# Seven products in place of eight for two blocks of each channel mixer in a four-layer decoder trunk

## The chip, the cores and the metric

The kernel runs on one core of one Trainium2 chip. The metric is device time in microseconds (us) of one launch. Five engines work from queues of their own: TensorE (PE in the profile; its weight loads are PEld), VectorE (DVE), ScalarE (ACT), GpSimd (POOL, unused here) and SyncE (SP), which issues the transfers. Each takes its instructions in the order in which the kernel recorded them.

## The reference

Four layers over 256 tokens of width 1024. Each has a mixer (retention, dilated attention, gated MLP, retention again), the channel mixer that the change touches, and a gated embedding:

```
FFN_HIDDEN = -(-(8 * D_MODEL) // (3 * 256)) * 256        # 2816
def _swiglu(h, w_in, w_out):
    gate, up = jnp.split(h @ w_in, 2, axis=-1)
    return (jax.nn.silu(gate) * up) @ w_out
...
    f = _swiglu(_rmsnorm(h, norm_g[i, 2]), ffn_w_in[i], ffn_w_out[i])
    h = h + _rmsnorm(f.astype(h.dtype), norm_g[i, 3])
```

All inputs are fp32.

## The kernel before

Every weight is streamed once, in "chunks" of at most 128x1024 fp32; a transfer brings two chunks (1 MB) into one of four raw buffers (`RAWS`). `split_one` splits a chunk into a high part `wh` (ScalarE copies it to fp32r, L172) and a low part `wl` (VectorE subtracts, L173). Eight split chunks can live at once (`SLOTS`). Each product is then three matmuls, `mm3` (L202 to L204): high by high, and the two crossed terms, the part not streamed being the activation's own split pair (`a_hi`, `a_lo`).

What order the work has is written by hand in the program (a manual schedule). When `Chunk` hands chunk c to TensorE's code, `tick` records the split of chunk c+6 (`LEAD`) at that place in ScalarE's and VectorE's queues.

In the channel mixer, `ffn`, the first 512 columns of gate and of up are computed token by feature, then turned by transposes (`turn`). The other 2304 columns of each go in nine "pairs" i = 2 to 10 of 256 columns: two gate chunks and two up chunks of 24 matmuls each, which stream the 256 tokens past weight blocks (`feature_major`), then `hidden` (silu(gate)*up and its split: L927, L928, L930, L933, L934), then two chunks of the output weight, `rows` of pair i-2, with 12 matmuls of 512 columns each into the accumulators `acc`.

Of the kernel before, what the change touches and what calls it, by code (L numbers as in the profile page):

```python
# [9 lines left out]
F32 = mybir.dt.float32  # L10
# [14 lines left out]
RAWS = 4  # L25
# [24 lines left out]
def _size(d):  # L50
    return d[3] * sum(n for _, n in d[4])


def _plan(l):
    kind, j = l % 3, l // 3
    emb = _rows("ple_w_proj", l, 0, 2)
    mix = []
    if kind == 0:
        for h in range(4):
            mix += _cols("ret_w_in", j, 2048 + 512 * h, 512, 2)  # L60
            mix += _blocks("ret_w_in", j, 256 * h, 2) + _blocks("ret_w_in", j, 1024 + 256 * h, 2)
# [20 lines left out]
    for i in range(2, NPAIR):  # L82
        mix += _blocks("ffn_w_in", l, 256 * i, 2) + _blocks("ffn_w_in", l, HID + 256 * i, 2)
        mix += _rows("ffn_w_out", l, 2 * i - 4, 2)
    mix += _rows("ffn_w_out", l, 2 * NPAIR - 4, 4)
    for q in range(2):
        mix += _cols("ple_w_gate", l, 512 * q, 512, 2)
    return mix


PLANS = [_plan(l) for l in range(DEPTH)]


def _pack(l, w):
# [12 lines left out]
def trunk(ctx: ExitStack, tc: tile.TileContext, x, p_t, norm_g, gcols, wts, rel_bias, gm_ln, gm_ws, gm_bs,  # L107
# [14 lines left out]
        return (psum if tag == "ps" else accp).tile([128, 512], F32, tag=tag, name=tag)  # L122


    chunks, groups = [], []
    for l in range(DEPTH):
        off = 0
        for d in PLANS[l]:
            n = _size(d)
            if len(chunks) % 2 == 0:  # L130
                groups.append((2 * n, wts[l][off:off + 256 * n].rearrange("(p n) -> p n", p=128)))
            assert 2 * n == groups[-1][0]
            chunks.append((d, n))
            off += 128 * n
    raws, slots, released = {}, {}, set()
    st = {"load": 0, "split": 0, "take": 0, "rate": 2}

    def load_to(i):
        while st["load"] <= min(i, len(groups) - 1):
# [4 lines left out]
            for cs in (slice(0, n // 2), slice(n // 2, n)) if g == 1 else (slice(0, n),) if g else ():  # L144
                dma.dma_start(out=t[:, cs], in_=src[:, cs])
            st["load"] += 1

# [16 lines left out]
    def split_one():  # L164
        c = st["split"]
        assert can_split()
        load_to(c // 2 + RAWS - 1)
        n = chunks[c][1]
        raw = raws[c // 2][:, c % 2 * n:(c % 2 + 1) * n]
# [15 lines left out]
    class Chunk:  # L185
        def __init__(self, name):
            c = st["take"]
            d, n = chunks[c]
# [9 lines left out]
            released.add(self.c)  # L198


    def mm3(ps, lh, ll, rh, rl, start, stop):
        pe.matmul(ps, lhsT=lh, rhs=rh, start=start, stop=False)  # L202
        pe.matmul(ps, lhsT=lh, rhs=rl, start=False, stop=False)  # L203
        pe.matmul(ps, lhsT=ll, rhs=rh, start=False, stop=stop)  # L204


    ident = const.tile([128, 128], F32, name="ident")
# [233 lines left out]
    def retention(l, r, between, env):  # L441
# [14 lines left out]
        for hd in range(4):  # L456
# [47 lines left out]
            def scores():  # L504
# [388 lines left out]
        return late, acc  # L893

    def rel_vectors(rp):
        rel = rp.tile([32, 48], F32, name="rel")
        hot = rp.tile([32, 3, 384], F32, name="hot")
        band = rp.tile([16, 3, 384], F32, name="band")
        sb = rp.tile([16, 3, 384], F32, name="relv")
        rh, rl = (rp.tile([32, 48], F32R, name=t) for t in ("relh", "rell"))  # L900
        dma.dma_start(out=rel, in_=rel_bias)
        dma.dma_start(out=hot, in_=c_onehot)
        dma.dma_start(out=band, in_=c_mask)

        def compute():
            hr = rp.tile([32, 3, 384], F32R, name="hotr")
            act.activation(out=hr, in_=hot, func=AF.Copy)
            act.activation(out=rh, in_=rel, func=AF.Copy)
            dve.tensor_tensor(out=rl, in0=rel, in1=rh.bitcast(F32), op=ALU.subtract)
            for g in range(3):  # L910
                ps = ps_tile()
                for i, part in enumerate((rh, rl)):
                    pe.matmul(ps[0:16, 0:384], lhsT=part[:, cut(g, 16)], rhs=hr[:, g, :], start=i == 0, stop=i == 1)
                dve.tensor_tensor(out=sb[:, g, :], in0=ps[0:16, 0:384], in1=band[:, g, :], op=ALU.add)  # L914
            dma.dma_start(out=vec.rearrange("g h u -> h g u"), in_=sb)

        return compute


    def ffn(l, r, between, env):  # L920
# [30 lines left out]
            return ps  # L951

        def first(tt, gp, up):
            s = fp.tile([128, 512], F32, tag="s0", name="s0")
# [7 lines left out]
        u1 = second_half(wu)  # L962
        first(1, g1, u1)
        st["rate"] = P["rate"]
        h0 = [fp.tile([128, 4, 256], F32R, tag=f"h0{i}", name="h0") for i in range(2)]
        acc = None
        for i in range(2, NPAIR):
            gp = feature_major(name)
            if i == 2:
                spread(r)  # L970
                for tt in range(2):
                    turn(hid0[tt], h0[0], h0[1], 0, tt)
                hids[0], hids[1] = (h0, 0), (h0, 2)
                gain = load_gain(l, 3)
                if l == 0:
                    rel_part = rel_vectors(fp)
            if i == 5 and l == 0:
                rel_part()
            up = feature_major(name)
            hidden(i, gp, up)  # L980
            if acc is None:
                acc = new_acc()
            late = []
            z, k0 = hids[i - 2]
            for k in range(2):
                c = Chunk(wout)
                if i < NPAIR - 1:
                    row(c, z, k0 + k, acc, i == 2 and k == 0, False)
                    c.release()
                else:  # L990
                    row(c, z, k0 + k, acc, False, False, (0,))
                    late.append((c, z, k0 + k))
        for i in range(NPAIR - 2, NPAIR):
            z, k0 = hids[i]
            for k in range(2):
                c = Chunk(wout)
                row(c, z, k0 + k, acc, False, i == NPAIR - 1 and k == 1, (0,))
                late.append((c, z, k0 + k))
        return close_branch(late, acc, gain, r, l, 4)

    def embed_gate(l, r, between):
# [59 lines left out]
    with tc.manual_schedule():  # L1061
        dma.dma_start(out=ident, in_=c_ident)
        for tt in range(2):
            dma.dma_start(out=h[:, tt, cut(0)], in_=x[tok(tt), cut(0)])
            if tt == 0:
                dma.dma_start(out=gc, in_=gcols)
        load_to(0)
# [5 lines left out]
        load_to(RAWS - 1)  # L1073
        dve.memset(ones, 1.0)
        dve.memset(eps, EPS)
        act.preload_act_table(AF.Sqrt)
# [102 lines left out]
```

## Time and profile before

| | |
|---|---|
| time, median of 3 runs | 1721.83 us (1721.56 to 1721.88) |
| the profiled execution | 1721.27 us, its span 1719.5 us |
| TensorE busy | 1708.8 us, 99% of the span |
| VectorE busy | 1138.7 us, 66% |
| ScalarE busy | 980.9 us, 57% |
| mean granted TensorE clock | 0.999 |

The span runs from the first to the last instruction; 1.8 us of the profiled execution lie outside it. Busy shares are averages over the whole program.

### The profile page before, as it was taken

How to read it: one execution, taken by the hardware profiler on the slowest of the kernel's cores; microseconds unless marked ns; L12 is line 12 of the kernel's file. 1: busy time of each engine (PE TensorE's matmuls, PEld its weight loads, DVE VectorE, ACT ScalarE, POOL GpSimd, SP SyncE). 2: the span in 40 equal slices, each digit the busy share in tenths (PEclk: the TensorE clock that was granted, in tenths of full speed). 3: DMA queues.
4: the chain of work that ended last, by engine and by line, in shares of the span. 5: the costliest groups of instructions: out<-in, count | busy, mean ns of one | idle time of the engine just before them, and what ended most of it. 6: DMA issues, size and time to landing. Idle time of an engine off the chain costs nothing.

```text
span 1719.5 us, 26156 instructions
## 1 busy us (share of the span) xinstructions
PE 1708.8 (99%) x10667; PEld 1543.6 (90%) x10667; DVE 1138.7 (66%) x1663; ACT 980.9 (57%) x1506; POOL 0.2 (0%) x4
## 2 busy tenths in 40 slices
PE   9999999999999999999999999999999999999999
PEld 7888899998999999799998888899988888889997
DVE  7666665557888888765557676755567665675556
ACT  6545764447777777754447644644457555764435
POOL 0000000000000000000000000000000000000000
PEclk9999999999999999999999999999999999999999
DMA  8544465553656556455554754565544544555550
GB/s 291 221 170 173 172 225 179 184 191 131 208 160 183 165 168 180 147 204 181 196 172 147 277 194 149 191 213 187 181 168 166 198 173 172 189 208 200 178 194 25
DMA packets 53593, 314.22 MB, mean 183 GB/s; under 512 B 5633, under 2 KB 13617, under 8 KB 19169
## 3 DMA queue, kind: packets, MB, share of 16 engines
q1 hardware_dynamic: 53472, 312.56, 53.0%
q8 instruction: 83, 1.36, 0.3%
q14 instruction: 38, 0.30, 0.1%
HBM read 311.41 MB, written 1.12 MB: 182 GB/s over the span
## 4 chain that ended last, share of the span: by engine, by line
PE 93%; DVE 3%; ACT 2%; issue 1%; DMA 0%; SPq 0%; ACTq 0%; DVEq 0%
PE ps L204 20%; PE ps L202 20%; PE ps L203 20%; PE acc L202 7%; PE acc L204 7%; PE acc L203 7%; PE ps L326 2%; DVE wl L173 2%; PE ps L322 2%; PE ps L323 2%; PE acc L260 1%; PE ps L251 1%; PE acc L635 1%; ACT wh L172 1%; PE acc L597 0%
## 5 line engine op out<-in xcount | busy, mean ns | idle before, releaser
L173 DVE TENSOR_TENSOR wl<-raw,wh 128x1024 fp32r<-128x1024 f32 (+1 forms) x567 | 660.9, 1205 | 197.9 <-ACT wh L172 197.1
L172 ACT ACTIVATE wh<-raw 128x1024 fp32r<-128x1024 f32 (+1 forms) x567 | 564.3, 1040 | 176.0 <-PE ps L203 106.8
L202 PE MATMUL ps<-a_hi,wh 128*128 128x256 f32 x1792 | 509.5, 284 | 0.0
L204 PE MATMUL ps<-a_hi,wl 128*128 128x256 f32 x1792 | 507.0, 283 | 0.0
L203 PE MATMUL ps<-a_lo,wh 128*128 128x256 f32 x1792 | 507.0, 283 | 0.0
L202 PEld LDWEIGHTS ps<-a_hi,wh 128*128 128x128 f32 x1792 | 343.6, 192 | 1.9 <-DVE relv L914 0.4
L203 PEld LDWEIGHTS ps<-a_lo,wh 128*128 128x128 f32 x1792 | 343.7, 192 | 1.5
L204 PEld LDWEIGHTS ps<-a_hi,wl 128*128 128x128 f32 x1792 | 343.6, 192 | 0.0
L202 PE MATMUL ps<-wh,a_hi 128*128 128x512 f32 (+2 forms) x632 | 240.1, 380 | 0.3 <-ACT wh L161 0.3
L204 PE MATMUL ps<-wh,a_lo 128*128 128x512 f32 (+2 forms) x632 | 238.3, 377 | 1.2 <-DVE a_lo L265 1.2
L203 PE MATMUL ps<-wl,a_hi 128*128 128x512 f32 (+2 forms) x632 | 238.3, 377 | 0.4 <-DVE wl L162 0.2
L204 PEld LDWEIGHTS ps<-wh,a_lo 128*128 128x128 f32 x632 | 118.7, 188 | 22.0 <-DVE a_lo L265 2.5
L202 PEld LDWEIGHTS ps<-wh,a_hi 128*128 128x128 f32 x632 | 118.8, 188 | 20.0 <-ACT wh L161 0.9
L203 PEld LDWEIGHTS ps<-wl,a_hi 128*128 128x128 f32 x632 | 118.9, 188 | 19.8 <-DVE wl L162 1.1
L202 PE MATMUL acc<-wh,hh 128*128 128x512 f32 x288 | 113.2, 393 | 0.0
L203 PE MATMUL acc<-wl,hh 128*128 128x512 f32 x288 | 112.8, 392 | 0.0
L204 PE MATMUL acc<-wh,hl 128*128 128x512 f32 x288 | 112.5, 391 | 0.0
L930 DVE TENSOR_TENSOR hid<-ps,gr 128x512 f32<-128x512 f32 x36 | 24.9, 691 | 99.4 <-PE ps L204 99.4
L933 ACT ACTIVATE hh<-hid 128x512 fp32r<-128x512 f32 x36 | 22.8, 632 | 101.5 <-DVE hid L930 101.5
L262 ACT ACTIVATE a_hi<-acc,gc 128x128 fp32r<-128x128 f32 x192 | 52.2, 382 | 42.9 <-PE acc L260 42.7
L204 PEld LDWEIGHTS acc<-wh,hl 128*128 128x128 f32 x288 | 54.1, 188 | 11.8
L202 PEld LDWEIGHTS acc<-wh,hh 128*128 128x128 f32 x288 | 54.2, 188 | 10.7
(208 smaller groups left out, 2087.9 us busy)
## 6 DMA issues: line engine op xcount, KB each, us to landing
raw<-in_w_dram SPq DMA_DIRECT2D x266, 1024.0 KB, 4.9
raw<-in_w_dram SPq DMA_DIRECT2D x16, 768.0 KB, 4.3
gain<-in_norm_g_dram SPq DMA_DIRECT2D x8, 512.0 KB, 6.5
bias<-vec SPq DMA_DIRECT2D x8, 384.0 KB, 7.0
emb<-vec SPq DMA_DIRECT2D x8, 384.0 KB, 8.6
ln<-in_gm_ln_dram SPq DMA_DIRECT2D x2, 1024.0 KB, 7.1
raw<-in_w_dram SPq DMA_DIRECT2D x3, 512.0 KB, 7.8
dec<-in_c_decay_dram SPq DMA_DIRECT2D x4, 384.0 KB, 5.4
```

The source lines that it names most:

```text
L172: act.activation(out=hi[:, 0:n], in_=raw, func=AF.Copy)
L173: dve.tensor_tensor(out=lo[:, 0:n], in0=raw, in1=hi[:, 0:n].bitcast(F32), op=ALU.subtract)
L202: pe.matmul(ps, lhsT=lh, rhs=rh, start=start, stop=False)
L203: pe.matmul(ps, lhsT=lh, rhs=rl, start=False, stop=False)
L204: pe.matmul(ps, lhsT=ll, rhs=rh, start=False, stop=stop)
L251: pe.transpose(ps[:, cut(i, 128)], src[:, cut(i, 128)], ident)
L262: act.activation(out=dst_hi[:, k0 + i, tok(tt)], in_=ps[:, cut(i, 128)], func=AF.Copy, scale=gain(k0 + i))
L322: pe.matmul(ps, lhsT=a, rhs=w.hi[:, k, :], start=kk == 0, stop=False)
L323: pe.matmul(ps, lhsT=a, rhs=w.lo[:, k, :], start=False, stop=False)
L326: pe.matmul(ps, lhsT=a_lo[:, kk, tok(tt)], rhs=w.hi[:, k, :], start=False, stop=kk == 7)
L930: dve.tensor_tensor(out=hd, in0=up, in1=gr, op=ALU.mult)
L933: act.activation(out=hh, in_=hd, func=AF.Copy)
```

## The change

In each layer the pairs 4 and 5 become one unit of 512 gate and 512 up columns, and so do the pairs 8 and 9: two units a layer, eight in all. A unit is a product of a 2x2 block matrix of activations (two tiles of 128 tokens, two halves of the 1024 inputs) by a 2x2 block matrix of weights (two halves of the inputs; gate and up), by Strassen's scheme in Winograd's form: seven block products of two chunks each.

- Four of the seven products take sums of weight blocks. Each is made by an added VectorE instruction ahead of the chunk's split, in place in the raw buffer: it adds another raw block (L202 of the changed kernel). A unit loads 8 chunks as before and splits 14, of which 8 with such an add. Its four raw buffers stay in use until their last reader; `load_more` waits for that.
- Four sums of activation blocks are made once a layer by `make_sums`, after pair 2.
- The products stand token by feature: each chunk serves one tile of 128 tokens, as 6 matmuls of 512 columns. The seven results are combined on VectorE (L1085, L1087, L1094, L1097, L1100), gated (L1098, L1102) and turned by 8 transposes in the next plain pair.
- `rel_vectors`, a small table for layer 1, moves from the first layer's channel mixer to its retention.

```diff
+    for i, seven in UNITS:
+        if seven:
+            plain(_rows("ffn_w_out", l, 2 * i - 4, 2))
+            e = len(mix)
+            g, u = _cols("ffn_w_in", l, 256 * i, 512, 2), _cols("ffn_w_in", l, HID + 256 * i, 512, 2)
+            mix += u[0:2] + g[0:2] + u[2:4] + g[2:4]
+            for at, add in ((2, None), (2, 0), (2, 4), (6, None), (0, 4), (4, None), (6, 2)):
+                uses += [(e + at + c, None if add is None else e + add + c) for c in range(2)]
+            plain(_rows("ffn_w_out", l, 2 * i - 2, 2))
...
+UNITS = ((2, False), (3, False), (4, True), (6, False), (7, False), (8, True), (10, False))
...
+    def load_more():
+        while st["load"] < len(groups):
             g = st["load"]
+            if g >= RAWS and last_use[g - RAWS] >= st["split"]:
+                break
...
+        raw = entry(chunks[c][2])
+        if chunks[c][3] is not None:
+            dve.tensor_tensor(out=raw, in0=raw, in1=entry(chunks[c][3]), op=ALU.add)
         hi = w_p.tile([128, 1024], F32R, tag="wh", name="wh")
         lo = w_p.tile([128, 1024], F32R, tag="wl", name="wl")
         act.activation(out=hi[:, 0:n], in_=raw, func=AF.Copy)
...
+            if l == 0 and hd == 1:
+                rel_part = rel_vectors(mp)
+            if l == 0 and hd == 2:
+                rel_part()
...
+        def whole(t, tt, half):
+            hi, lo = block(tt, half)
+            dve.tensor_tensor(out=k4(t), in0=hi.bitcast(F32), in1=lo.bitcast(F32), op=ALU.add)
+            return t
+
+        def split_sum(n, t):
+            act.activation(out=sums[n][0], in_=k4(t), func=AF.Copy)
+            dve.tensor_tensor(out=sums[n][1], in0=k4(t), in1=sums[n][0].bitcast(F32), op=ALU.subtract)
...
+        def make_sums():
+            t21, t22 = whole(flat("gr"), 1, 0), whole(pn(), 1, 1)
+            s1 = flat("hid")
+            dve.tensor_tensor(out=s1, in0=t22, in1=t21, op=ALU.subtract)
+            split_sum(0, s1)
+            t11 = whole(flat("gr"), 0, 0)
+            s2 = pn()
+            dve.scalar_tensor_tensor(out=s2, in0=s1, scalar=-1.0, in1=t11, op0=ALU.mult, op1=ALU.subtract)
+            split_sum(1, s2)
...
+        def seven(i):
...
+            def prod(ps, a, start=True, more=False):
+                for c in range(2):
+                    w = Chunk(name)
+                    for k in range(2):
+                        kk = 2 * c + k
+                        mm3(ps, a[0][:, kk, :], a[1][:, kk, :], w.hi[:, k, :], w.lo[:, k, :], start and kk == 0,
+                            kk == 3, more)
+                    w.release()
...
+            p1 = ps_tile()
+            prod(p1, block(0, 0))
+            u2 = flat("gr")
+            act.activation(out=u2, in_=p1, func=AF.Copy)
+            p5 = ps_tile()
+            prod(p5, sums[0])
+            p6 = ps_tile()
+            prod(p6, sums[1])
+            dve.tensor_tensor(out=u2, in0=p6, in1=u2, op=ALU.add)
+            u4 = flat("gr")
+            dve.tensor_tensor(out=u4, in0=p5, in1=u2, op=ALU.add)
+            prod(p1, block(0, 1), False, True)
+            s = [fp.tile([128, 512], F32, tag="s0", name="s0", bufs=2) for _ in range(2)]
+            act.activation(out=s[0], in_=p1, func=AF.Silu, scale=r[0])
+            p7 = ps_tile()
+            prod(p7, sums[2])
+            up1 = flat("hid")
+            dve.tensor_tensor(out=up1, in0=p7, in1=u4, op=ALU.add)
+            p3 = ps_tile()
+            prod(p3, sums[3])
+            dve.tensor_tensor(out=u4, in0=p3, in1=u4, op=ALU.add)
+            dve.scalar_tensor_tensor(out=hid0[0], in0=u4, scalar=-1.0, in1=s[0], op0=ALU.mult, op1=ALU.mult)
+            prod(p7, block(1, 1), False, True)
+            dve.tensor_tensor(out=u2, in0=p7, in1=u2, op=ALU.add)
+            act.activation(out=s[1], in_=u2, func=AF.Silu, scale=r[1])
+            dve.scalar_tensor_tensor(out=hid0[1], in0=up1, scalar=-1.0, in1=s[1], op0=ALU.mult, op1=ALU.mult)
+            todo.append(i)
...
+        for i, is_seven in UNITS:
+            if is_seven:
+                rows(i - 2)
+                seven(i)
+                rows(i - 1)
+                continue
```

VectorE's queue before, at one plain pair (here pair 3 of the first layer): the low parts of six chunks (two stand here) and `hidden`. Row names are line, operation, output<-inputs and shape.

```order
L927 TENSOR_TENSOR gr_2515<-ps_2397,r_b_88 128x512
L930 TENSOR_TENSOR hid_2518<-ps_2456,gr_2515 128x512
L934 TENSOR_TENSOR hl_2521<-hid_2518,hh_2520 128x512
L173 TENSOR_TENSOR wl_2527<-raw_2363,wh_2526 128x1024
L173 TENSOR_TENSOR wl_2543<-raw_2363,wh_2542 128x1024
```

The same engine and place in the changed kernel: behind `hidden` of pair 3 (now L964, L967, L971) come the chunks of the unit's second and third product.

```order
L964 TENSOR_TENSOR gr_2562<-ps_2444,r_b_88 128x512
L967 TENSOR_TENSOR hid_2565<-ps_2503,gr_2562 128x512
L971 TENSOR_TENSOR hl_2568<-hid_2565,hh_2567 128x512
L202 TENSOR_TENSOR raw_2410<-raw_2410,raw_2314 128x1024
L206 TENSOR_TENSOR wl_2573<-raw_2410,wh_2572 128x1024
L202 TENSOR_TENSOR raw_2410<-raw_2410,raw_2314 128x1024
L206 TENSOR_TENSOR wl_2590<-raw_2410,wh_2589 128x1024
```

Ahead of each low part stands an add into the raw buffer from which ScalarE then makes the high part that the low part's instruction reads.

The third place is VectorE's queue at the end of the same unit, from the sixth product's chunks (`raw_2445`) over the seventh's (`raw_2504`) to the two chunks of `rows(3)` behind the unit (`raw_2686`).

```order
L206 TENSOR_TENSOR wl_2689<-raw_2445,wh_2688 128x1024
L206 TENSOR_TENSOR wl_2699<-raw_2445,wh_2698 128x1024
L1085 TENSOR_TENSOR gr_2660<-ps_2685,gr_2660 128x512
L1087 TENSOR_TENSOR gr_2709<-ps_2662,gr_2660 128x512
L202 TENSOR_TENSOR raw_2504<-raw_2504,raw_2410 128x1024
L206 TENSOR_TENSOR wl_2713<-raw_2504,wh_2712 128x1024
L202 TENSOR_TENSOR raw_2504<-raw_2504,raw_2410 128x1024
L206 TENSOR_TENSOR wl_2724<-raw_2504,wh_2723 128x1024
L206 TENSOR_TENSOR wl_2744<-raw_2686,wh_2743 128x1024
L206 TENSOR_TENSOR wl_2754<-raw_2686,wh_2753 128x1024
L1094 TENSOR_TENSOR hid_2763<-ps_2736,gr_2709 128x512
```

L1094 reads the fifth product (`ps_2736`) and stands behind every split up to `rows(3)`. On TensorE, the last matmuls of the sixth product and the first of the seventh in this unit:

```order
L235 MATMUL ps_2765<-wh_2698,s3h_2236 128x512
L236 MATMUL ps_2765<-wl_2699,s3h_2236 128x512
L237 MATMUL ps_2765<-wh_2698,s3l_2237 128x512
L235 MATMUL ps_2736<-wh_2712,a_hi_83 128x512
L236 MATMUL ps_2736<-wl_2713,a_hi_83 128x512
L237 MATMUL ps_2736<-wh_2712,a_lo_84 128x512
```

The seventh product accumulates on top of the fifth in the same PSUM tile, `ps_2736`, so its first matmul follows L1094's reading. All eight units have these orders.

## Rows read from the trace of the kernel before

**Rows 1.** The page: busy time by engine, and the chain that ended last.
```profile
PE 1708.8 (99%) x10667; PEld 1543.6 (90%) x10667; DVE 1138.7 (66%) x1663; ACT 980.9 (57%) x1506; POOL 0.2 (0%) x4
PE 93%; DVE 3%; ACT 2%; issue 1%; DMA 0%; SPq 0%; ACTq 0%; DVEq 0%
```
**Rows 2.** Waits of TensorE: who for whom, us in total, times, longest.
```profile
PE ps L1084 <- DVE warm L1079: 1.5, 1, 1.5
PE ps L322 <- ACT a_hi L262: 1.2, 1, 1.2
```
**Rows 3.** Timeline, TensorE, one pair: start us, us, instruction.
```profile
304.75 0.40 PE L204 MATMUL acc<-wh,hl 128*128 128x512 f32 x1
304.99 0.28 PE L202 MATMUL ps<-a_hi,wh 128*128 128x256 f32 x1
...
316.36 0.28 PE L204 MATMUL ps<-a_hi,wl 128*128 128x256 f32 x1
316.48 0.40 PE L202 MATMUL acc<-wh,hh 128*128 128x512 f32 x1
```
**Rows 4.** Stretches (gate+up, rows, pair): busy PE, PEld, DVE, ACT, POOL; clock; DMA.
```profile
304.99:316.48 11.49, 11.49 (x97) 11.49 (x96) 4.78 (x5) 3.81 (x4) 0.00 (x0) 1.00 0.75 243
299.38:304.99 5.61, 5.61 (x27) 4.52 (x26) 4.38 (x5) 3.48 (x4) 0.00 (x0) 1.00 0.40 162
299.30:316.40 17.10, 17.10 (x123) 16.01 (x122) 9.15 (x9) 7.29 (x8) 0.00 (x0) 1.00 0.64 218
```
**Rows 5.** Timeline, TensorE: the eight transposes of the first 512 columns.
```profile
240.36 1.04 PE L251 MATMUL ps<-ident,hid 128*128 128x128 f32 x8
241.16 0.36 PE L202 MATMUL ps<-a_hi,wh 128*128 128x256 f32 x1
```
**Rows 6.** Timeline, VectorE, the pair of rows 3; idle time before in brackets.
```profile
301.99 3.50 DVE L173 TENSOR_TENSOR wl<-raw,wh 128x1024 fp32r<-128x1024 f32 x3 [0.26 <-ACT wh L172]
306.34 1.23 DVE L173 TENSOR_TENSOR wl<-raw,wh 128x1024 fp32r<-128x1024 f32 x1 [0.85 <-ACT wh L172]
...
313.10 0.68 DVE L927 TENSOR_TENSOR gr<-ps,r_b 128x512 f32<-128x512 f32 x1
316.75 0.69 DVE L930 TENSOR_TENSOR hid<-ps,gr 128x512 f32<-128x512 f32 x1 [2.97 <-PE ps L204]
318.14 0.69 DVE L934 TENSOR_TENSOR hl<-hid,hh 128x512 fp32r<-128x512 f32 x1 [0.70 <-ACT hh L933]
```
**Rows 7.** Timeline, ScalarE, the same pair.
```profile
305.25 1.06 ACT L172 ACTIVATE wh<-raw 128x1024 fp32r<-128x1024 f32 x1 [1.39 <-PE acc L204]
...
313.82 0.63 ACT L928 ACTIVATE gr<-gr 128x512 f32<-128x512 f32 x1 [1.89 <-DVE gr L927]
317.48 0.63 ACT L933 ACTIVATE hh<-hid 128x512 fp32r<-128x512 f32 x1 [3.03 <-DVE hid L930]
```
**Rows 8.** Groups by line and shape, VectorE: busy us, mean ns, idle before.
```profile
L173 DVE TENSOR_TENSOR wl<-raw,wh 128x1024 fp32r<-128x1024 f32 x535 | 631.4, 1220 | 194.7 <-ACT wh L172 193.9
L404 DVE TENSOR_TENSOR h<-h,pn 128x512 f32<-128x512 f32 x32 | 22.1, 692 | 1.1
```
**Rows 9.** DMA issues: times, KB each, median us to landing.
```profile
raw<-in_w_dram SPq DMA_DIRECT2D x266, 1024.0 KB, 4.9
```
**Rows 10.** Timeline, TensorE's weight loads, the program's first matmuls.
```profile
1.91 0.15 PEld L1084 LDWEIGHTS <-warm 128*128 128x128 bf16 x1 [0.28 <-issue]
2.34 0.15 PEld L1084 LDWEIGHTS <-warm 128*128 128x128 bf16 x1 [0.28 <-issue]
```
**Rows 11.** Those matmuls by line: ns min/median/max, first and last start.
```profile
L1084 PE MATMUL ps<-warm x9: 407/634/634, 1.5 to 7.4; 128*128 128x512 bf16 x9
```
**Rows 12.** L914 of `rel_vectors` by line: who waited for it.
```profile
  PEld ps L202: 0.4, 1
```

More of the change, by code (lines that the diff above doesn't have):

```diff
@@ L81, in _plan, with plain @@
     mix += _cols("ffn_w_in", l, 0, 512, 2) + _cols("ffn_w_in", l, HID, 512, 2)
[L82 to L85, printed above, removed]
+    uses = [(e, None) for e in range(len(mix))]
+    def plain(ds):
+        uses.extend((len(mix) + i, None) for i in range(len(ds)))
+        mix.extend(ds)
+    for i, seven in UNITS:
[7 more added lines that the diff above has]
+            plain(_rows("ffn_w_out", l, 2 * i - 2, 2))
+        else:
+            plain(_blocks("ffn_w_in", l, 256 * i, 2) + _blocks("ffn_w_in", l, HID + 256 * i, 2))
+            plain(_rows("ffn_w_out", l, 2 * i - 4, 2))
+    plain(_rows("ffn_w_out", l, 2 * NPAIR - 4, 4))
     for q in range(2):
-        mix += _cols("ple_w_gate", l, 512 * q, 512, 2)
-    return mix
-PLANS = [_plan(l) for l in range(DEPTH)]
+        plain(_cols("ple_w_gate", l, 512 * q, 512, 2))
+    return mix, uses
+UNITS = ((2, False), (3, False), (4, True), (6, False), (7, False), (8, True), (10, False))
+PLANS, USES = zip(*[_plan(l) for l in range(DEPTH)])
 def _pack(l, w):
@@ L122, in ps_tile @@
         return (psum if tag == "ps" else accp).tile([128, 512], F32, tag=tag, name=tag)
-    chunks, groups = [], []
+    chunks, groups, last_use = [], [], {}
+    entries = 0
     for l in range(DEPTH):
         off = 0
-        for d in PLANS[l]:
+        for i, d in enumerate(PLANS[l]):
             n = _size(d)
-            if len(chunks) % 2 == 0:
+            if (entries + i) % 2 == 0:
                 groups.append((2 * n, wts[l][off:off + 256 * n].rearrange("(p n) -> p n", p=128)))
             assert 2 * n == groups[-1][0]
-            chunks.append((d, n))
             off += 128 * n
+        for e, add in USES[l]:
+            for i in (e, add):
+                if i is not None:
+                    last_use[(entries + i) // 2] = len(chunks)
+            chunks.append((PLANS[l][e], _size(PLANS[l][e]), entries + e, None if add is None else entries + add))
+        entries += len(PLANS[l])
     raws, slots, released = {}, {}, set()
     st = {"load": 0, "split": 0, "take": 0, "rate": 2}
-    def load_to(i):
-        while st["load"] <= min(i, len(groups) - 1):
+    def load_more():
+        while st["load"] < len(groups):
             g = st["load"]
+            if g >= RAWS and last_use[g - RAWS] >= st["split"]:
+                break
             n, src = groups[g]
@@ L143, in load_to @@
             raws[g] = t
-            for cs in (slice(0, n // 2), slice(n // 2, n)) if g == 1 else (slice(0, n),) if g else ():
+            for cs in (slice(0, n // 2), slice(n // 2, n)) if g == 1 else (slice(0, n),):
                 dma.dma_start(out=t[:, cs], in_=src[:, cs])
@@ L166, in split_one, with entry @@
         assert can_split()
-        load_to(c // 2 + RAWS - 1)
+        load_more()
         n = chunks[c][1]
-        raw = raws[c // 2][:, c % 2 * n:(c % 2 + 1) * n]
+        def entry(e):
+            return raws[e // 2][:, e % 2 * n:(e % 2 + 1) * n]
+        raw = entry(chunks[c][2])
+        if chunks[c][3] is not None:
+            dve.tensor_tensor(out=raw, in0=raw, in1=entry(chunks[c][3]), op=ALU.add)
         hi = w_p.tile([128, 1024], F32R, tag="wh", name="wh")
@@ L187, in __init__ @@
             c = st["take"]
-            d, n = chunks[c]
+            d, n = chunks[c][0:2]
             assert d[0] == name, (d, name)
@@ L198, in release, with mm3 @@
             released.add(self.c)
[L201 to L204, printed above, removed]
+    def mm3(ps, lh, ll, rh, rl, start, stop, more=False):
+        pe.matmul(ps, lhsT=lh, rhs=rh, start=start, stop=False, skip_group_check=more)
+        pe.matmul(ps, lhsT=lh, rhs=rl, start=False, stop=False, skip_group_check=more)
+        pe.matmul(ps, lhsT=ll, rhs=rh, start=False, stop=stop, skip_group_check=more)
     ident = const.tile([128, 128], F32, name="ident")
@@ L895, in rel_vectors @@
     def rel_vectors(rp):
-        rel = rp.tile([32, 48], F32, name="rel")
-        hot = rp.tile([32, 3, 384], F32, name="hot")
+        room = emb.rearrange("p a b -> p (a b)")[0:32, :]
+        hot, rel = room[:, 0:1152].rearrange("p (g u) -> p g u", g=3), room[:, 1152:1200]
         band = rp.tile([16, 3, 384], F32, name="band")
-        sb = rp.tile([16, 3, 384], F32, name="relv")
         rh, rl = (rp.tile([32, 48], F32R, name=t) for t in ("relh", "rell"))
@@ L913, in compute @@
                     pe.matmul(ps[0:16, 0:384], lhsT=part[:, cut(g, 16)], rhs=hr[:, g, :], start=i == 0, stop=i == 1)
-                dve.tensor_tensor(out=sb[:, g, :], in0=ps[0:16, 0:384], in1=band[:, g, :], op=ALU.add)
-            dma.dma_start(out=vec.rearrange("g h u -> h g u"), in_=sb)
+                dve.tensor_tensor(out=band[:, g, :], in0=ps[0:16, 0:384], in1=band[:, g, :], op=ALU.add)
+            dma.dma_start(out=vec.rearrange("g h u -> h g u"), in_=band)
         return compute
@@ L953, in first @@
         def first(tt, gp, up):
-            s = fp.tile([128, 512], F32, tag="s0", name="s0")
+            s = fp.tile([128, 512], F32, tag="s0", name="s0", bufs=2)
             act.activation(out=s, in_=gp, func=AF.Silu, scale=r[tt])
@@ L964, in ffn, with flat, turn_hid @@
         st["rate"] = P["rate"]
-        h0 = [fp.tile([128, 4, 256], F32R, tag=f"h0{i}", name="h0") for i in range(2)]
-        acc = None
-        for i in range(2, NPAIR):
+        acc, late, todo = [], [], []
+        def flat(tag):
+            t = fp.tile([128, 2, 256], F32, tag=tag, name=tag, bufs=2)
+            return t.rearrange("p a b -> p (a b)")
+        def turn_hid(i):
+            h0 = [fp.tile([128, 4, 256], F32R, tag=f"h0{k}", name="h0") for k in range(2)]
+            for tt in range(2):
+                turn(hid0[tt], h0[0], h0[1], 0, tt)
+            hids[i], hids[i + 1] = (h0, 0), (h0, 2)
@@ new lines, in rows @@
+        def rows(i, tail=False):
+            if not acc:
+                acc.extend(new_acc())
+            z, k0 = hids[i]
+            for k in range(2):
+                c = Chunk(wout)
+                row(c, z, k0 + k, acc, i == 0 and k == 0, i == NPAIR - 1 and k == 1, (0,) if tail else (0, 1))
+                if tail:
+                    late.append((c, z, k0 + k))
+                else:
+                    c.release()
+        sums = [[fp.tile([128, 4, 128], F32R, name=f"s{n}{p}") for p in "hl"] for n in range(4)]
@@ new lines, in block, with k4 @@
+        def block(tt, half):
+            return [t[:, 4 * half:4 * half + 4, tok(tt)] for t in (a_hi, a_lo)]
+        def k4(t):
+            return t.rearrange("p (k t) -> p k t", k=4)
+        def whole(t, tt, half):
[5 more added lines that the diff above has]
+            dve.tensor_tensor(out=sums[n][1], in0=k4(t), in1=sums[n][0].bitcast(F32), op=ALU.subtract)
@@ new lines, in pn @@
+        def pn():
+            return tmp_p.tile([128, 512], F32, tag="pn", name="pn")
+        def make_sums():
[7 more added lines that the diff above has]
+            split_sum(1, s2)
+            s3 = pn()
+            dve.tensor_tensor(out=s3, in0=t11, in1=t21, op=ALU.subtract)
+            split_sum(2, s3)
+            t12 = whole(pn(), 0, 1)
+            dve.tensor_tensor(out=t12, in0=t11, in1=t12, op=ALU.subtract)
+            s4 = pn()
+            dve.tensor_tensor(out=s4, in0=t12, in1=s1, op=ALU.add)
+            split_sum(3, s4)
@@ new lines, in seven @@
+        def seven(i):
+            def prod(ps, a, start=True, more=False):
+                for c in range(2):
+                    w = Chunk(name)
+                    for k in range(2):
+                        kk = 2 * c + k
[29 more added lines that the diff above has]
+            todo.append(i)
@@ L970, in ffn @@
                 spread(r)
-                for tt in range(2):
-                    turn(hid0[tt], h0[0], h0[1], 0, tt)
-                hids[0], hids[1] = (h0, 0), (h0, 2)
+            if todo:
+                turn_hid(todo.pop())
+            if i == 2:
                 gain = load_gain(l, 3)
[L975 to L978, printed above, removed]
             up = feature_major(name)
             hidden(i, gp, up)
[L981 to L992, printed above, removed]
-        for i in range(NPAIR - 2, NPAIR):
[L994 to L998, printed above, removed]
+            if i == 2:
+                make_sums()
+            rows(i - 2, i == NPAIR - 1)
+        for i in range(NPAIR - 2, NPAIR):
+            rows(i, True)
         return close_branch(late, acc, gain, r, l, 4)
@@ L1066, in trunk @@
                 dma.dma_start(out=gc, in_=gcols)
-        load_to(0)
+        n, src = groups[0]
+        raws[0] = raw_p.tile([128, 2048], F32, tag="raw", name="raw")
+        st["load"] = 1
         for i in range(2):
@@ L1072, in trunk @@
             dma.dma_start(out=h[:, tt, cut(1)], in_=x[tok(tt), cut(1)])
-        load_to(RAWS - 1)
+        load_more()
         dve.memset(ones, 1.0)
```

1 line of the change is left out of this document (added).

## The prediction, made before the changed kernel ran

> **What bounds the kernel now.** I read the page first: TensorE is busy for 99% of the span and holds 93% of the chain that ended last; VectorE has 66% [rows 1]. The list of TensorE's waits says that this is no average over good and bad stages: the longest wait in the program is 1.5 us, at its start, and the next 1.2 us [rows 2]. So a matmul saved is time saved, as long as TensorE goes on finding its chunks split. Whether it does is read from one pair, where the change is made. The next matmul starts when the last has streamed, so durations overlap and spacing is what counts: gate and up are 96 matmuls in 316.48 - 304.99 = 11.49 us [rows 3, 4], 0.1197 us each; `rows` are 24 of 512 columns in 5.61 us [rows 4], 0.234 each. A pair is 17.1 us, of which VectorE is busy for 9.15 [rows 4]. It has slack because its splits wait for slots that TensorE frees: in the pair most low parts wait for ScalarE's copy, and that copy for TensorE [rows 6, 7]. The splits run six chunks ahead of use. A chunk is worth 2.8 us of TensorE (24 x 0.1197, or 12 x 0.234) and 1.14 us of VectorE ((3.50 - 1.22)/2 between three back to back [rows 6, 8]).
>
> **What is saved on TensorE.** A unit takes the place of 192 matmuls of 256 columns (192 x 0.1197 = 22.98 us) with 84 of 512 (84 x 0.234 = 19.66). In return 8 transposes come with the turn; eight took 241.16 - 240.36 = 0.80 us [rows 5]. Net 2.52 us a unit, 20.2 us for eight units, if nothing waits. Most of it is the eighth product, 12 x 0.234 = 2.8 us.
>
> **What is added on VectorE and ScalarE.** In a unit a chunk lasts only 6 x 0.234 = 1.40 us on TensorE, since it serves one token tile. VectorE needs 1.14 us for a plain split, and far more for one with an add. No row shows the add at 128x1024. Its nearest rows are the low part's subtraction of the same shape, also of two fp32 operands from SBUF, 1.22 us, and an in-place add of half the width, 0.692 us [rows 8]: so 1.22, and not under 1.14. The order shows add, then split, and the split's ScalarE copy reads what the add writes. The three form a chain in which VectorE's queue stands: add 1.22, hand-over 0.04 (L927 ends 313.78, L928 starts 313.82), copy 1.06, hand-over 0.03 (306.31 to 306.34), then 1.14 until the next instruction can start [rows 6, 7]: 3.49 us a chunk against TensorE's 1.40. Eight such chunks are 27.9 us, while the whole unit is worth 19.66 us of TensorE.
>
> **One unit, walked through.** Let 0 be the time at which TensorE could start the unit's first chunk. Pair 3's up ends two `rows` earlier, at -11.23. L930 starts 0.27 after such an end and L934 1.39 later [rows 3, 6]; with 0.65 for L934 (0.69 less the overlap with the next), the add of the second product's first chunk starts at -8.9. The first product's two chunks were split before. VectorE's queue from there, each time when the next instruction can start:
> - second and third product, four chunks with add: 4 x 3.49, to 5.0. Fourth product, two plain: to 7.3. Fifth, two with add: to 14.3. Sixth, two plain: to 16.6;
> - L1085 and L1087, 0.7 each: to 18.0. Seventh product, two with add: to 25.0;
> - the two chunks of `rows(3)`: to 27.2; then L1094, done at 27.9.
>
> TensorE, fed by that: the third product's second chunk waits little, the fifth's second chunk has its low part at 14.4, the sixth product starts when L1085 has read its PSUM tile, at 17.3, and ends at 20.1. Then comes the worst place: the seventh product goes on top of the fifth in one PSUM tile, L1094 must have read it, and L1094 stands behind four splits that TensorE doesn't need yet. It starts at 28.0 and ends at 30.8 in place of 19.7. **Lost: 11.1 us a unit**, with one gap of 7.9 us. Behind that, `rows(3)` is split already, and the turn (L1102 at about 36) is wanted at 42, so nothing more is lost. The six chunks of lead are used up in this: what was ahead at -8.9 is in the sum.
>
> The first unit of a layer starts later. `make_sums` puts 13 instructions of about 0.69 us and four waits of 0.70 for ScalarE (as L934's [rows 6]) into VectorE's queue, 11.8 us. After pair 2 the queue is then: 2.3 until L934 is through, 11.8, 0.4 for the first copy, six splits 6.8, `hidden` of pair 3 3.4; together 24.7. TensorE reaches the unit 11.49 + 3 x 5.61 = 28.3 after pair 2's up. So the first add starts at -3.6, 5.3 later than above, and the chain shifts with it: 16.4 us lost. The chunks ahead cover the rest: the first of `rows(1)` is ready at 15.6 and wanted at 17.1.
>
> **Transfers.** 1 MB lands 4.9 us after its issue [rows 9]. The unit's first buffer comes free when the fifth product is split, at 14.4; its refill is there at 19.3 and is wanted from 25.0. The next three are issued at 16.7, about 23 and 25.1 and wanted by VectorE at 28, 32 and 36: covered by 2 us or more. Without that cover each us late would be a us for VectorE, and 8 us over the units.
>
> **The table for layer 1.** Its matmuls, adds and transfers are the same ones in another place. Where they stand now TensorE waited 0.4 us for them [rows 12]; I take 0, within 1 us either way.
>
> **TensorE's clock.** In this trace it never stood for more than 1.5 us after its first matmul, and the granted clock in the pair is 1.00 [rows 2, 4]. The one place where it works after standing still is the program's start: the weight loads of 512-column matmuls are 0.43 us apart [rows 10], which is 512 columns at 1.2 GHz, the lower level, and the matmuls take 634 ns, the last one, at 7.4 us, 407 [rows 11]. So it took 5.9 us from the first matmul at 1.5 us to full speed. A gap of 7.9 us lies between these two cases. Bounds per unit: 0, and half of 5.9, 2.9 us. I take the start as the nearer in kind, since 7.9 us is five times the longest gap that did no harm, and 2.5 us, 13 matmuls of 0.193 us more each (0.427 against 0.234): 20 us in all. The Trainium skill has a rule for it, in "TensorE: Matmul & The Clock Gate", "HAM oscillation — how this bites in real kernels": matmuls behind a long wait run cold, and pay again after each such wait. By that rule the unit pays as in my sum; by the pair's row alone, clock 1.00 throughout, it pays nothing and the sum is 20 us less.
>
> **The sum.** Gain 20.2; lost 4 x (16.4 + 11.1) = 110.0; clock 20. Together +109.8 us on the profiled execution's 1721.27, so 1831 us. The median of the three runs is 0.56 us above that execution, which is less than anything here.
>
> **The rivals.**
> *The clock stays.* The same waits, and TensorE at full speed behind them: 1721.3 - 20.2 + 110 = 1811. For it speaks that 1.00 is all that the trace shows in mid-program; against it the start.
> *The lead covers the chain: faster.* If the add's chain overlapped in VectorE's queue, or the adds ran well ahead, a unit would keep its 2.52 us: 1701. It decides at 2.52 us lost a unit: below that the kernel gains. For it speaks that VectorE's own work in a unit with its `rows`, 26 instructions of 1.14 and seven of about 0.7, is 35 us against 31 of TensorE, an excess that the six chunks ahead could bear if nothing waited inside a chain. Against it speaks the order: nothing stands between an add and its split.
> *Transfers are late too.* Three transfers come out of buffers held to the unit's end. At twice the landing time, 9.8 us, the third and fourth refill (wanted 9 and 11 us after issue) come about as they are wanted; at three times the splits wait some 5 us a unit more, 40 us: 1871. The pair moves 218 GB/s on average and its DMA engines are 64% busy [rows 4], which leaves room; a landing in between gives 1835 to 1855.
> *Only part of the walk is right.* If the adds ran at 1.0 us and the hand-overs cost nothing, a unit's 8 chains would be 2.3 us shorter; with a clock that falls in every other unit, some 1803.
>
> **How the numbers follow.** Chances: my forecast 0.58 (its own range 1818 to 1845), the clock stays 0.20, late transfers 0.11, a part 0.06, the lead covers it 0.05. The range from 1798 to 1856 takes in the first two with their bounds, the part, and late transfers that cost up to 3 us a unit; left out are the faster case and the worst of the transfers. A measurement of this kernel can tell about 0.2% (3.4 us) from no change. Faster 0.05, the same 0.02 (a loss of 2.1 to 2.9 us a unit), slower 0.93.
>
> **What would show it.** In the changed kernel's profile: TensorE waiting for L1094 eight times, some 8 us each, as the longest entry of its waits; low parts of chunks with an add waiting about 1.1 us for ScalarE, 64 times; L202 at 1.22 us; VectorE's busy time up by about 8 x (6 + 8) x 1.2 + 4 x 9 = 170 us while TensorE's share falls below 95%; four of the eight units 5 us longer than the others; half-speed matmuls (634 ns in place of 393) right behind each wait. I am wrong if the adds start much before pair 3's `hidden` is through, if L1094's wait is missing, or if the clock is 1.00 behind gaps of 8 us.

## The result, and the profile after

The changed kernel takes 1842.95 us (median of 4 runs, 1842.38 to 1843.80) against 1721.74 of the kernel before: a ratio of 1.0704, interval 1.0686 to 1.0723. The forecast was 1831, range 1798 to 1856.

The page of the changed kernel: busy time by engine, the granted TensorE clock in tenths over 40 slices of the span, and the chain that ended last, to be read against [rows 1].

```profile
span 1840.6 us, 24853 instructions
PE 1733.3 (94%) x9867; PEld 1514.0 (82%) x9867; DVE 1313.2 (71%) x1851; ACT 1037.9 (56%) x1578; POOL 0.2 (0%) x4
PEclk9999998989999999998989999999899999998989
PE 74%; DVE 12%; ACT 7%; issue 4%; DMA 1%; SPq 0%; ACTq 0%; DVEq 0%
L202 DVE TENSOR_TENSOR raw<-raw 128x1024 f32<-128x1024 f32 x64 | 77.9, 1218 | 0.0
```

TensorE has 800 matmuls fewer and yet more busy time, since part of it runs at half clock; VectorE and ScalarE, which had 5% of the chain, now have 19%. Each of the seven 8s in the clock's row stands at a unit; the remaining unit, the first of the third layer, is spread over two slices and shows none. The waits of TensorE in the changed kernel, in total, times, longest, answer to [rows 2].

```profile
PE ps L235 <- DVE hid L1094: 53.5, 8, 8.1
PE ps L236 <- DVE wl L206: 14.9, 22, 0.8
PE ps L235 <- ACT wh L205: 12.9, 18, 0.9
PE ps L235 <- DVE gr L1085: 9.8, 8, 1.5
PE ps L950 <- ACT relh L945: 4.3, 1, 4.3
```

L1094 is waited for eight times, as the walk had it, for 5.9 to 8.1 us each. The second unit of the first layer starts on TensorE at 369.23. VectorE's queue around it, by time, with the idle time before an instruction in brackets (some rows left out):

```profile
360.60 1.22 DVE L202 TENSOR_TENSOR raw<-raw 128x1024 f32<-128x1024 f32 x1
363.02 1.23 DVE L206 TENSOR_TENSOR wl<-raw,wh 128x1024 fp32r<-128x1024 f32 x1 [1.21 <-ACT wh L205]
364.16 1.22 DVE L202 TENSOR_TENSOR raw<-raw 128x1024 f32<-128x1024 f32 x1
...
391.38 1.22 DVE L202 TENSOR_TENSOR raw<-raw 128x1024 f32<-128x1024 f32 x1
393.80 1.23 DVE L206 TENSOR_TENSOR wl<-raw,wh 128x1024 fp32r<-128x1024 f32 x1 [1.20 <-ACT wh L205]
395.32 2.36 DVE L206 TENSOR_TENSOR wl<-raw,wh 128x1024 fp32r<-128x1024 f32 x2 [0.29 <-ACT wh L205]
397.60 0.68 DVE L1094 TENSOR_TENSOR hid<-ps,gr 128x512 f32<-128x512 f32 x1
```

One chunk with an add holds VectorE from 360.60 to 364.16, 3.56 us, 1.21 of it waiting for ScalarE's copy. The first add starts 8.6 us before the unit (forecast 8.9), L1094 is through 29.0 after it (27.9). TensorE at the end of the sixth product and across the gap:

```profile
390.87 0.60 PE L237 MATMUL ps<-wh,s3l 128*128 128x512 f32 x1
391.30 0.41 PE L235 MATMUL ps<-wh,s3h 128*128 128x512 f32 x1
...
398.42 0.77 PE L235 MATMUL ps<-wh,a_hi 128*128 128x512 f32 x1 [6.25 <-DVE hid L1094]
398.99 0.63 PE L236 MATMUL ps<-wl,a_hi 128*128 128x512 f32 x1
399.42 0.63 PE L237 MATMUL ps<-wh,a_lo 128*128 128x512 f32 x1
...
401.55 0.39 PE L236 MATMUL ps<-wl,a_hi 128*128 128x512 f32 x1
```

The matmul at 398.42 is the seventh product's first; 0.63 us and a spacing of 0.43 are half clock. The same stretch by busy time of the engines (PE, PEld, DVE, ACT, POOL), then granted clock, DMA share, GB/s; the last row is the first unit of that layer.

```profile
384.49:391.30 6.81, 6.27 (x15) 4.43 (x16) 5.57 (x6) 1.51 (x2) 0.00 (x0) 0.50 0.85 308
398.40:402.71 4.31, 4.29 (x13) 3.42 (x14) 4.28 (x5) 1.62 (x2) 0.00 (x0) 0.64 1.01 382
369.23:402.70 33.47, 24.76 (x85) 18.43 (x84) 26.20 (x25) 16.71 (x18) 0.00 (x0) 0.80 0.44 163
284.43:323.52 39.09, 25.08 (x85) 17.96 (x84) 30.34 (x30) 18.05 (x19) 0.00 (x0) 0.83 0.38 146
```

A unit with nothing to wait for takes 19.04 us (the first experiment). The second units of the four layers took 33.4 to 33.9 us, the first ones 38.8 to 39.6, all eight together 291.4.

### The profile page after: what moved, and what is told of

It reads as the page before. It is cut to its first block, busy times and chain, and to the rows that moved or that the text cites. A ratio compares the mean times of both kernels' runs of the same rounds, so it can differ in the third digit from the quotient of the medians.

```text
span 1840.6 us, 24853 instructions
## 1 busy us (share of the span) xinstructions
PE 1733.3 (94%) x9867; PEld 1514.0 (82%) x9867; DVE 1313.2 (71%) x1851; ACT 1037.9 (56%) x1578; POOL 0.2 (0%) x4
## 4 chain that ended last, share of the span: by engine, by line
PE 74%; DVE 12%; ACT 7%; issue 4%; DMA 1%; SPq 0%; ACTq 0%; DVEq 0%
PE ps L235 16%; PE ps L237 16%; PE ps L236 16%; PE acc L235 6%; PE acc L237 6%; PE acc L236 6%; DVE wl L206 6%; ACT wh L205 5%; DVE raw L202 3%; PE ps L359 1%; PE ps L355 1%; PE ps L356 1%; PE ps L284 1%; DMA raw<-in_w_dram 1%; PE acc L293 1%
## 5 line engine op out<-in xcount | busy, mean ns | idle before, releaser
L206 DVE TENSOR_TENSOR wl<-raw,wh 128x1024 fp32r<-128x1024 f32 x615 | 715.3, 1206 | 169.1 <-ACT wh L205 167.0
L205 ACT ACTIVATE wh<-raw 128x1024 fp32r<-128x1024 f32 x615 | 608.5, 1040 | 216.2 <-DVE raw L202 139.5
L235 PE MATMUL ps<-a_hi,wh 128*128 128x256 f32 x1280 | 365.6, 286 | 0.0
L237 PE MATMUL ps<-a_hi,wl 128*128 128x256 f32 x1280 | 362.5, 283 | 0.0
L236 PE MATMUL ps<-a_lo,wh 128*128 128x256 f32 x1280 | 362.4, 283 | 0.0
L236 PEld LDWEIGHTS ps<-a_lo,wh 128*128 128x128 f32 x1280 | 245.7, 192 | 0.9
L235 PEld LDWEIGHTS ps<-a_hi,wh 128*128 128x128 f32 x1280 | 245.6, 192 | 0.9
L237 PEld LDWEIGHTS ps<-a_hi,wl 128*128 128x128 f32 x1280 | 245.6, 192 | 0.0
L236 PEld LDWEIGHTS ps<-wl,a_hi 128*128 128x128 f32 x728 | 142.1, 195 | 25.1 <-DVE wl L189 1.1
L202 DVE TENSOR_TENSOR raw<-raw 128x1024 f32<-128x1024 f32 x64 | 77.9, 1218 | 0.0
L235 PE MATMUL acc<-wh,h 128*128 128x512 f32 x192 | 75.0, 391 | 0.0
L237 PE MATMUL acc<-wh,h 128*128 128x512 f32 x192 | 74.8, 389 | 0.0
```

What stands on the lines that cost most here:

```text
L202: dve.tensor_tensor(out=raw, in0=raw, in1=entry(chunks[c][3]), op=ALU.add)
L235: pe.matmul(ps, lhsT=lh, rhs=rh, start=start, stop=False, skip_group_check=more)
L236: pe.matmul(ps, lhsT=lh, rhs=rl, start=False, stop=False, skip_group_check=more)
L237: pe.matmul(ps, lhsT=ll, rhs=rh, start=False, stop=stop, skip_group_check=more)
```

## The experiments

The theory is that of the forecast: VectorE's chain of add, copy and subtraction delays the seventh product's chunks, L1094's place behind four splits adds to it, and half clock comes on top. The rivals stand with each run. "Time" is the median on the chip; the kernel before had 1720.8 to 1722.6 us beside these runs.

**The adds left out.** The weight sums are not formed in this run.

```diff
-        if chunks[c][3] is not None:
-            dve.tensor_tensor(out=raw, in0=raw, in1=entry(chunks[c][3]), op=ALU.add)
```

> The 64 adds of weight blocks are left out (the weight sums are not formed, so the products are other ones); all 14 splits of a unit, all matmuls, the PSUM tile shared by two products and the transfers stay. Theory (the chain add, copy, subtraction holds VectorE's queue): each of the eight chunks costs VectorE 1.14 us in place of 3.57, L1094 comes before the fifth product is done, the units lose nothing: 1721 - 20 + 8 (the table for layer 1) = 1709 us, and the granted clock stays at 1.0 in the units. Rival 1 (the six more splits or the raw buffers held long are what delays): most of the loss stays, above 1800. Rival 2 (the shared PSUM tile by itself): the waits for L1094 stay, 8 times, at several us.

Time 1701.95 us (one run). No wait for L1094 is left, and the unit (rows as above, the layer's first and second unit) is TensorE's alone:

```profile
283.46:302.50 19.04, 19.04 (x86) 15.77 (x84) 18.09 (x19) 14.34 (x16) 0.00 (x0) 1.00 0.72 266
348.20:367.24 19.04, 19.04 (x86) 15.77 (x84) 15.67 (x16) 13.95 (x15) 0.00 (x0) 1.00 0.62 238
```

So splits, buffers, transfers and the shared tile lose nothing without the adds. It came out 7 us below the expectation: 5 of them because 84 matmuls take 19.04 us, 0.2267 each, and not 0.234, and most of the rest because the expectation had 8 us for the table for layer 1 (5, see below).

**Adds one chunk ahead.** The low part waits in a list until the next split; nothing is left out. A raw buffer counts as free only when its low part is recorded.

```diff
-            if g >= RAWS and last_use[g - RAWS] >= st["split"]:
+            if g >= RAWS and last_use[g - RAWS] >= st["split"] - len(pending):
...
+    pending = []
+    def lows():
+        while pending:
+            lo, raw, hi = pending.pop(0)
+            dve.tensor_tensor(out=lo, in0=raw, in1=hi.bitcast(F32), op=ALU.subtract)
...
-        dve.tensor_tensor(out=lo[:, 0:n], in0=raw, in1=hi[:, 0:n].bitcast(F32), op=ALU.subtract)
+        lows()
+        pending.append((lo[:, 0:n], raw, hi[:, 0:n]))
+        if chunks[c][3] is None:
+            lows()
```

> The same instructions, but the low part of a chunk with an add is recorded one split later, behind the next chunk's add, so that ScalarE's copy runs while VectorE adds. Theory (the chain's waiting, not the amount of VectorE's work): such a chunk costs 2.28 us in place of 3.57, L1094 starts at 17.9 us after the unit's start in place of 28.4 (23.0 in place of 33.4 in a layer's first unit), lost per unit 2 and 7 us: 1721 - 20 + 8 + 35 = 1744, up to 1756 with half clock behind the first units' gaps. Rival (VectorE has too much work, however ordered): less than a third of the loss goes, above 1810.

Time 1768.16 us (one run): 75 of the 121 us are gone with the same instructions in another order. VectorE in the second unit of the first layer, to be held against the rows of the changed kernel:

```profile
351.50 2.35 DVE L209 TENSOR_TENSOR raw<-raw 128x1024 f32<-128x1024 f32 x2
353.92 1.23 DVE L196 TENSOR_TENSOR wl<-raw,wh 128x1024 fp32r<-128x1024 f32 x1
355.18 1.23 DVE L209 TENSOR_TENSOR raw<-raw 128x1024 f32<-128x1024 f32 x1
356.32 1.22 DVE L196 TENSOR_TENSOR wl<-raw,wh 128x1024 fp32r<-128x1024 f32 x1
```

A chunk with an add now takes 2.4 us, with no bracket. So the rival (too much work, however ordered) fell. The expectation was 12 us too low at its upper end: in this unit L1094 started 1 us later than worked out, and TensorE still waited 35.9 us for it over the eight units, with half clock behind seven of the eight gaps and not behind four.

**A PSUM tile for the seventh product.**

```diff
+            dve.tensor_tensor(out=u2, in0=p7, in1=u2, op=ALU.add)
...
-            prod(p7, block(1, 1), False, True)
-            dve.tensor_tensor(out=u2, in0=p7, in1=u2, op=ALU.add)
+            p4 = ps_tile()
+            prod(p4, block(1, 1))
+            dve.tensor_tensor(out=u2, in0=p4, in1=u2, op=ALU.add)
```

> The seventh product gets a PSUM tile of its own and is added on VectorE by one more instruction of 0.69 us a unit, so that its first matmul no longer follows L1094. The chains stay. Theory (two causes in series: the chain sets when the seventh product's low parts are there, at 22.2 and 25.8 us after the unit's start, and L1094 adds the splits of the next two chunks on top): the unit's last matmul ends at 27.2 to 28.4 in place of 33.5, 5 to 6 us a unit: 1843 - 45 = 1798, and the longest gap of TensorE falls below 3.5 us. Rival (the shared tile is the whole loss): 1709 to 1720. Rival (the shared tile is only where the wait shows): no change, 1843.

Time 1789.95 us (one run), 53 less, and the longest wait of TensorE in a unit is 1.5 us. But a unit still takes 32.1 and 27.1 us:

```profile
285.14:317.27 32.13, 25.97 (x85) 18.45 (x84) 23.42 (x22) 14.23 (x16) 0.00 (x0) 0.84 0.25 96
363.17:390.28 27.11, 21.26 (x86) 15.37 (x84) 19.88 (x18) 13.04 (x15) 0.00 (x0) 1.00 0.31 112
```

The shared tile is a cause of its own, not only the place where the wait shows, and not the whole of it: the loss has two causes in series, of which this removes one. The gains of this run and of the one before, 53 and 75 us, do not add up to the loss of 121, because both shorten the wait for L1094.

**The table's copies earlier.** In the changed kernel the copies of the table for layer 1 (L944, L945) stand behind L524 on ScalarE, which follows a rope step (L518 to L521) that reads the product TensorE has just ended, and TensorE's next matmul (L950) needs them:

```profile
120.09 0.28 PE L237 MATMUL ps<-a_hi,wl 128*128 128x256 f32 x1
120.66 0.68 DVE L518 TENSOR_TENSOR ta<-ps,turned 128x512 f32<-128x512 f32 x1
122.77 0.63 ACT L524 ACTIVATE qkh<-ta 128x512 fp32r<-128x512 f32 x1 [3.47 <-DVE ta L521]
124.36 0.23 ACT L945 ACTIVATE relh<-emb 32x48 fp32r<-32x48 f32 x1
124.64 0.34 PE L950 MATMUL ps<-hotr,relh 32*16 32x384 f32 x1 [4.27 <-ACT relh L945]
```

In this run `compute` is cut in two: its copies (L944 to L946) are recorded at the start of the third head, its matmuls stay.

```diff
+            if l == 0 and hd == 2:
+                rel_part[0]()
             if hd:
                 token_major(name, ev_v)
...
-                rel_part()
+                rel_part[1]()
...
```

> The copies of the table for layer 1 (L944 to L946) are recorded at the start of the third head of layer 0's retention, its matmuls stay where they are. Theory (TensorE waits 4.3 us for these copies, which stand behind a rope step on ScalarE, and then works at half clock for 6.8 us, 3.4 us lost): 7.7 us less than the changed kernel, 1835. Rival (the 8 us that the forecast's terms leave open come from the units): 1842 to 1843.

Time 1838.6 us (2 runs), 4.3 less than the changed kernel. The 4.3 us wait is gone, and the first unit starts at 279.16 in place of 284.43, 5.3 us earlier. Of the other 2.4 us of the 7.7, 1.5 came back as two waits of TensorE in the same place that the changed kernel does not have (0.9 us for L951's adds into the table, 0.6 for a rope step).

**The gap filled.**

```diff
+            idle = ps_tile()
+            for _ in range(24):
+                pe.matmul(idle, lhsT=a_hi[:, 0, 0:128], rhs=a_hi[:, 0:2, :].rearrange("p k t -> p (k t)"), start=True, stop=True)
             prod(p7, block(1, 1), False, True)
```

> 24 matmuls of 512 columns that nothing reads (5.4 us at full clock) stand on TensorE between the sixth and the seventh product of each unit, inside the gap before L1094's end. Theory (the gap is set by VectorE, and half clock behind it costs about 2 us a unit, worked out from the unit's times): TensorE works at 2.4 GHz behind the gap, 16 us less than the changed kernel, 1827, and L1094 starts where it did. Rival (half clock is a large part of the loss: the records show 117 us of it): 1790 to 1800. Rival (VectorE in its turn waits for TensorE, so that more work there lengthens the unit): above 1843.

Time 1832.2 us (2 runs), 10.7 less, with 192 matmuls more. First and second unit:

```profile
283.05:321.62 38.57, 29.95 (x110) 22.01 (x109) 29.81 (x29) 18.05 (x19) 0.00 (x0) 0.91 0.39 143
367.43:399.47 32.04, 28.57 (x110) 21.69 (x109) 24.77 (x24) 16.72 (x18) 0.00 (x0) 0.89 0.41 158
```

The second units, at full clock behind the filled gap, all take 32.0 us, 1.3 to 1.8 less than in the changed kernel. Of the first units one stayed at full clock there and took 37.0; in the other three a fall remained, and they took 38.5 to 38.7. The changed kernel's eight units are 291.4 us together; with 32.0 and 37.0 for all they would be 276, so half clock behind the gap costs it 15 us, as far as the one first unit stands for the four. The records of the changed kernel show 117 us of half clock, but most of that time costs nothing, because TensorE then waits anyway.

**The first unit one pair later.**

```diff
-UNITS = ((2, False), (3, False), (4, True), (6, False), (7, False), (8, True), (10, False))
+UNITS = ((2, False), (3, False), (4, False), (5, True), (7, False), (8, True), (10, False))
```

> The first unit of a layer takes the pairs 5 and 6 in place of 4 and 5, so that one more plain pair stands between the sums of activation blocks and the unit, and one less between the two units. Theory (make_sums puts VectorE 5 us behind at the first unit): the first units lose what the second do, 14.5 in place of 20.3 us each, 4 x 5.8 = 23 us less than the changed kernel: 1820. Rival (first units lose more for another reason, such as the PSUM or the transfers of the gain): 1843. Rival (one plain pair between the units is too little for VectorE to catch up): the second units lose more, 1830 or above.

Time 1822.5 us (one run), 20.4 less. Both units of the first layer:

```profile
301.12:335.47 34.35, 22.77 (x85) 17.18 (x84) 27.08 (x26) 16.72 (x18) 0.00 (x0) 0.85 0.44 170
364.23:397.82 33.59, 24.75 (x86) 18.49 (x84) 26.32 (x25) 16.72 (x18) 0.00 (x0) 0.80 0.43 166
```

They are alike now (33.4 to 34.5 us in all four layers), so the first units' 5 us were `make_sums` in VectorE's queue; one plain pair between the units is enough.

**All four.** The four diffs of adds ahead, own tile, table early and later unit together.

> All four together: adds one chunk ahead of the low parts, a PSUM tile for the seventh product, the table's copies early, the first unit one pair later. Theory: the low parts of the seventh product are there at 15.2 us after a unit's start and wanted at 16.3, so that no unit waits; the eight units keep their 22.98 - 19.04 - 0.80 = 3.14 us, 25 us in all: 1696 to 1703, faster than both kernels, granted clock 0.99 or more. Rival (VectorE's work in a unit, some 35 us against 30 us of TensorE, is too much even so): units lose 2 us or more each, 1715 or above.

Time 1696.56 us (4 runs), a ratio of 0.9856 to the kernel before, interval 0.984 to 0.9873: faster than both kernels, than the kernel before by 1.4%. Its busy times, and two units:

```profile
PE 1682.7 (99%) x9867; PEld 1493.1 (88%) x9867; DVE 1313.5 (78%) x1859; ACT 1036.4 (61%) x1578; POOL 0.2 (0%) x4
295.14:314.18 19.04, 19.04 (x86) 15.77 (x85) 18.59 (x18) 12.43 (x14) 0.00 (x0) 1.00 0.50 188
342.90:361.94 19.04, 19.04 (x86) 15.77 (x85) 18.52 (x18) 12.44 (x14) 0.00 (x0) 1.00 0.47 172
```

VectorE is as busy as in the changed kernel, 1313 us, and in a unit for 98% of the time: the amount of its work was not the cause.

**Adds ahead and the tile, without the other two diffs.**

> Adds one chunk ahead and a PSUM tile for the seventh product; the table and the first unit stay where the changed kernel has them. Theory: second units lose nothing, first units, 5 us later on VectorE, about 4 us each; table 4 to 8: 1721 - 25 + 17 + 6 = 1719. Rival (the order alone was enough for the second units, and first units are bound by make_sums in another way): within 3 us of the run with all four.

Time 1720.1 us (one run), the kernel before within 0.1%. Second units lose nothing, first units 3.9 us each:

```profile
285.90:308.87 22.97, 20.16 (x86) 15.53 (x84) 22.38 (x22) 13.48 (x15) 0.00 (x0) 1.00 0.36 136
354.60:373.64 19.04, 19.04 (x86) 15.77 (x85) 18.59 (x18) 12.43 (x14) 0.00 (x0) 1.00 0.50 187
```

So `make_sums` (4 x 3.9 = 16 us) and the table (5 us) take 21 of the 25 us gained.

**Eight products in the new layout.** Each chunk serves both token tiles, without any sums; table early and later unit stay.

```diff
...
+            def ev_g(tt, ps):
+                act.activation(out=s[tt], in_=ps, func=AF.Silu, scale=r[tt])
+            def ev_u(tt, ps):
+                dve.tensor_tensor(out=hid0[tt], in0=ps, in1=s[tt], op=ALU.mult)
+            token_major(name, ev_g)
+            token_major(name, ev_u)
...
```

> The same two blocks a layer, token by feature and with the turn as in the run with all four, but as eight block products: each of the eight chunks serves both token tiles with 12 matmuls, no weight or activation sums, 8 splits a unit. Theory (the gain of the run with all four is the product left out, not the other layout): a unit takes 96 x 0.2267 + 0.80 = 22.6 us against 22.98 before, 0.4 us a unit: 1717 to 1719, with no waits of TensorE in the units. Rival (the layout gives most of it): 1700 or below.

Time 1719.5 us (8 runs), ratio 0.9989 (0.9978 to 1.0001). Each unit's 96 matmuls take 21.76 us, as worked out. It is 23 us slower than the run with all four, and 12 matmuls of 0.2267 us in eight units are 21.8: nearly all of the gain is the product left out, and hardly any the layout.

## Why the prediction was right

The walk through one unit held: the cause, its place (L1094 behind four splits), the 5 us of `make_sums` at the first units, and a fall of the clock behind the wait. The gaps were 6.7 us on average and not 7.9, since the sixth product ran at half clock already (in the unit above it ended 2.7 us later than worked out); this earlier fall was not foreseen. The sizes of the terms, measured against 1721.7:

- **Saved on TensorE**: forecast 20.2, measured 25.1 us (8 x (22.98 - 19.04 - 0.80)). The spacing of 0.234 was read from one `rows` stretch [rows 4]; most matmuls of 512 columns stand 0.2267 apart, about four in five already in the trace of the kernel before, among them those of the units' form (`ps<-wh,a_hi`), which was the nearer row.
- **Lost in the units by waits**: forecast 110, measured 124 us (4 x (32.0 + 37.0 - 2 x 19.04), from the run with the gap filled). The chain takes 3.56 us and not 3.49, the copies of the two chunks of `rows` cost 0.29 more, the unit is shorter by 0.6 without waits, and the hand-over to TensorE was not in the sum.
- **Half clock**: forecast 20, measured 15 us, some 2 a unit (from the run with the gap filled). In "HAM oscillation — how this bites in real kernels" of the page "TensorE: Matmul & The Clock Gate" the Trainium skill says that matmuls behind a long wait run cold (at half clock) each time. The trace agrees behind all eight waits for L1094: in the unit above the granted clock is 0.64 over the seventh product, whose matmuls start 0.43 us apart until 401.55.
- **The table for layer 1**: forecast 0 within 1, measured 5 us (the first unit's start in the run with the copies earlier). This step failed. "The same ones in another place" overlooked what they stand behind there: ScalarE's copies come after a rope step that waits for TensorE's last product, and TensorE's next instruction needs the copies.

-25 + 124 + 15 + 5 = +119; measured +121. The errors of the first two terms are in part one error (0.234 against 0.2267, in both) and cancel there. That half clock came out 5 us smaller and the table 5 us larger than forecast cancels by luck.

The rivals: the clock did not stay (the run with the gap filled tells its price), the lead did not cover the chain as built, and no transfer was late: the median landing was still 4.9 us, the slowest around a unit 7.3, and no engine waits for a weight transfer after the first 280 us (of the 1% of DMA in the chain, 12 us lie at the program's start and 6 in the last unit, where VectorE and ScalarE show no wait for it and which took 33.6 us like its fellows). The faster rival named what was missing, adds ahead of the low parts: with that and three more edits the kernel takes 1697 us, where it gave 1701.

## What to carry to other kernels

Trading a matmul for vector work is priced by the queue, not by the busy share: VectorE had a third of its time free, and yet a chunk with an add cost it 2.4 us more than a plain split, half of that (1.21 us) because the subtraction behind the add waited for another engine's copy of the add's result. Put the next item's first step ahead of the present one's last, and keep the instruction that frees a PSUM tile ahead of work that is not yet needed. A gain of 3 us a unit bears no slip elsewhere: with the order and the tile put right, the table's place (5 us) and `make_sums` (16 us) still ate nearly all of it.

## What was not expected of the hardware

In every unit of the changed kernel the clock fell to half already ahead of the long gap. In the second unit of the first layer it fell at 384.5, at the end of this stretch, with TensorE busy for 13.3 of the 15.3 us and no single wait above 0.9 us:

```profile
369.23:384.49 15.26, 13.34 (x57) 10.20 (x56) 10.77 (x10) 7.89 (x9) 0.00 (x0) 1.00 0.00 0
```

That fall cost nothing in this unit, because TensorE then waited for L1094 anyway, and VectorE's queue ahead of L1094 waited for ScalarE alone; why the clock fell there is left open. And matmuls of 512 columns stand 0.2267 us apart in some stretches and 0.234 in others at the same granted clock of 1.00; why is left open too.
